# Turning the values of two recurrences with VectorE's 32x32 blocks instead of TensorE, in a fused hybrid decoder layer

## The chip, the cores and the metric

One core of a Trainium2 chip runs the whole layer as one program. The metric is device time in microseconds (us). A time is that of one execution; the kernel before has three, and the profile is of a further execution of its own.

## What is computed

One layer over 320 tokens: 256 of a new sequence (the prompt) and 64 sampled ones (8 requests of 8 tokens), all in float32, with D_MODEL = 2048. Cut to what matters:

```python
proj = jnp.einsum('btd,de->bte', x, w_in)                # all head groups and gates in one projection
h, C, n, m = _mlstm(q, k, v, ig, lf, C0, n0, m0)          # 4 heads, DK 256, DV 512
#   num = einsum('bhts,bhsv->bhtv', s, v) + w_inter * einsum('bhtk,bhkv->bhtv', q, C)
#   den = sum(s) + w_inter * einsum('bhtk,bhk->bht', q, n)
#   C_new = decay * C + einsum('bhs,bhsk,bhsv->bhkv', w_end, k, v)
o, S = _hgrn2(hq, log(f), 1 - f, i, S0)                   # 8 heads, DK 128, DV 256
ya, yb = branch_a @ w_branch_a, branch_b @ w_branch_b
mix = (sig(gate_a) * ya + sig(gate_b) * yb) @ w_out
x1 = layernorm(alpha * x + mix)
y = layernorm(alpha * x1 + relu(x1 @ w_up) ** 2 @ w_down)
```

The outputs are y and the new states C, n, m and S, of the prompt and of the samples.

## The kernel before, in words

**Main stream.** All big projections are one stream of 304 output tiles of 128 columns (`TILES`, made by `tile_list`): the mLSTM projections (v, k, q of a head, between them gates), the HGRN2 projections, then output gates, branches, w_out, and four rounds of w_up and w_down. A tile is [128 columns x 320 tokens] in one PSUM bank and takes 16 steps of 128 along the contraction. Each step is three float32r matmuls (hi x hi, hi x lo, lo x hi: weights and activations are split into a high and a low part), so 48 matmuls to a tile; a half tile of 24 is a unit. Everything is transposed: features lie on partitions, tokens along the free dimension.

**Weights.** `prep` brings a unit of weights from its DMA buffer: ScalarE writes the high part (line 346, `wh<-wr` or `bb<-wr`) and VectorE the low part (line 491). The parts lie in buffer pairs: three at first, eight from w_out on (five wide ones in `bb`); one of the wide ones is lent to the first layer norm meanwhile.

**Recurrences.** Each mLSTM head and each HGRN2 head is a handful of small chains (Python generators): scores, values, states, numerator, samples. The matmuls that contract over tokens need the values with tokens on partitions. So `m_V` turns an mLSTM head's values (128 features x 4 blocks x 320 tokens) by 12 TensorE transposes into PSUM (line 954), from which ScalarE and VectorE make high and low parts; `h_i` turns an HGRN2 head's by 6 (lines 1465 and 1470). The 64 sampled tokens are turned along with the 64 last ones of the prompt, so that they land on partitions 64 to 127. Denominators of the mLSTM are sums over partitions, made as [128 x 1] matmuls with a column of ones (`m_num`, `m_sample`).

**What sets the order.** `Sched` is a planner in Python that runs while the program is built. It has a clock per engine and a cost for each instruction (`act`, `dve`, `pe_r`, `PE_T`), and between the main matmuls `pump` issues the next instruction of any chain whose inputs will be there by its clocks. An instruction of a chain on TensorE goes out only when its input will have been ready for 590 ns by these clocks (`LAT` and `PE_LAT`); VectorE's and ScalarE's at most 900 ns ahead. The result is a fixed order on each engine; on the chip an engine that comes to an instruction too early waits there.

**The end.** After the last tile of w_down come the second layer norm and the prompt's states. `ln_pre` sums the statistics of the first 15 tiles by float32 matmuls with ones (line 352, `bank<-f,ones`) while the last tile runs; `ln_final` adds the last tile; `ln_scale` makes mean M and the factor RS (lines 1838 to 1846 on VectorE, a logarithm and an exponential on ScalarE); `y` subtracts M (line 1960), multiplies by RS (line 1965), ScalarE applies weight and bias (`yb_`, `f3m<-f3m,vec`), and SyncE sends y off. Beside this run the states' matmuls: eight groups of six for C (`m_C`), whose k and v come back from HBM into freed weight buffers through GpSimd's DMA queue (line 1110), and eight pairs for S (`h_S`), each copied out by ScalarE or VectorE.

**Buffers.** SBUF is carved by hand from a few big tiles (`carve`, `carve_h`); regions are reused as stages end.

Of the kernel before, what the change touches and what calls it, by code (L numbers as in the profile page):

```python
# [20 lines left out]
TOK = 320  # L21
# [246 lines left out]

def pe_f(n, m=128):
    return max(212.0 if m == 128 else 162.0, n * 1.66)  # L270
# [39 lines left out]
class Program:  # L310
# [48 lines left out]
    def carve(self):  # L359
# [15 lines left out]
        self.hs = Pool([A(2048) for _ in range(3)])  # L375
# [15 lines left out]
        self.tst = Pool([B(320) for _ in range(2)])  # L391
# [26 lines left out]
        B = Part(self.f2, 4304)  # L418
# [7 lines left out]
    def carve_h(self):  # L426
        C = self.Part(self.pool.tile([128, 5120], F32, name="f3h", tag="f3"))
        qz = C(256)
        self.hqz = Pool([qz])
        self.hyk = Pool([C(128)])  # L430
        for x in (qz, self.ats0, self.hkz0.bitcast(F32), *(y[0:64, 2, :] for y in self.it2)):
            self.nc.gpsimd.memset(x, 0.0)
        X, R = self.Part(self.pool.tile([128, 4096], F32R, name="rxb", tag="rx")), self.Part(self.ra)
        self.bah = Slices([(X if j < 12 else R)(TOK) for j in range(KT)])
        self.bal = Slices([R(TOK) for _ in range(KT)])
        now = self.s.t["pe"]
        self.hs.free.append((now, C(2048)))
# [331 lines left out]
    def rows(self, b):  # L769
# [6 lines left out]
        ig, fx, ax, e, u, lnu, c1, r, lf, bb, a, a1, mt, em = (row() for _ in range(14))  # L776
# [136 lines left out]
    def m_S(self, h):  # L913
# [23 lines left out]
        yield ("act", act(256), lambda: self.A(ss[0:64], f(ss[64:128])))  # L937
        yield post(m["S"])

    def m_V(self, h):  # L940
        nc, v, m = self.nc, self.nc.vector, self.mh[h]
        if h:
            yield wait(self.mh[h - 1]["vst"])
        yield wait(*m["v"])
        vr = m["vr"]
        vhl = yield acq(self.vhl)
        m["vhl"] = vhl
        vh, vl = vhl[:, 0], vhl[:, 1]
        vs = yield acq(self.vs)
        m["vs"] = vs  # L950
        for i, lo in enumerate((0, 128, 192)):
            b = yield acq(self.sbank)
            for j in range(4):
                yield ("pe", PE_T, lambda: nc.tensor.transpose(b[:, 128 * j:128 * j + 128], vr[:, j, lo:lo + 128], self.ident))  # L954

            hi, lo_, x = (vh[:, i, :], vl[:, i, :], b) if i < 2 else (vs[64:128], vs[0:64], b[64:128])
            yield ("act", act(512, True), lambda: self.A(hi, x))
            yield ("dve", dve(512, True), lambda: v.tensor_tensor(lo_, x, hi.bitcast(F32), ALU.subtract))
            yield rel(self.sbank, b)
        yield rel(self.vr, vr)  # L960
# [23 lines left out]
    def m_KW(self, h):  # L984
# [15 lines left out]
        yield ("dve", dve(512), lambda: v.transpose(kw[:, :, 0:256], kw[:, :, 0:256]))  # L1000
# [58 lines left out]
    def m_num(self, h):  # L1059
# [13 lines left out]
        yield ("pe", 212, lambda: self.mm(db[:, 1:2], E[:, 128:256], one, start=True, stop=False))  # L1073
        yield ("pe", 212, lambda: self.mm(db[:, 1:2], E[:, 256:384], one, start=False, stop=True))
        for i in range(2):
            b = yield acq(self.sbank)
            jobs = [(c, s) for c, s in (((0, 0),), ((128, 0), (256, 1)))[i]]
            n = 0
            for c, s in jobs:
                for x, w in ((sh, vh), (sh, vl), (sl, vh)):  # L1080
                    st, sp = n == 0, n == 3 * len(jobs) - 1
                    yield ("pe", pe_r(512), lambda: self.mm(b, x[:, c:c + 128], w[:, s, :], start=st, stop=sp))
                    n += 1
            yield from self.ln_post(h, i, b, db[:, i:i + 1], hb[:, i, :], 128, True)
            yield rel(self.sbank, b)
            yield ("dve", dve(512), lambda: v.transpose(hb[:, i, :], hb[:, i, :]))
# [18 lines left out]
    def m_C(self, h):  # L1105
# [8 lines left out]
        for c in range(2):  # L1114
            if h:
                yield wait(self.ln[1]["fin"])
# [6 lines left out]
            if h < 2 and c == 0:  # L1123
                yield ("dve", dve(512, True), lambda: self.nc.vector.tensor_copy(self.oC[h][:, c, :], b))
            else:
                yield ("act", act(512, True), lambda: self.A(self.oC[h][:, c, :], b))
            yield rel(self.mbank, b)
            yield ("sp", 620, lambda: self.dma(self.d["Cp"][h, :, c, :], self.oC[h][:, c, :]))
        yield rel(self.vx, w)

# [14 lines left out]
    def m_sample(self, h):  # L1145
# [8 lines left out]
        for c in range(2):  # L1154
# [3 lines left out]
            yield ("dve", dve(64), lambda: v.tensor_tensor(by_token(qn, 128 * c, True), qc, n4, ALU.mult))  # L1158
        yield post(m["QW"])
# [13 lines left out]
        for i in range(2):  # L1173
            yield ("pe", pe_r(512), lambda: self.mm(nb, ss[:, 128 * i:128 * i + 128], m["vs"], start=False, stop=i == 1, skip_group_check=True))
        db = yield acq(self.sbank)
        yield ("pe", 212, lambda: self.mm(db[:, 0:1], E[:, 384:512], self.one, start=True, stop=False))
        for c in range(2):
            yield ("pe", 212, lambda: self.mm(db[:, 0:1], qn[:, 128 * c:128 * c + 128], self.one, start=False, stop=c == 1))
# [274 lines left out]
    def h_i(self, h):  # L1453
# [8 lines left out]
        b = yield acq(self.sbank)  # L1462
# [3 lines left out]
        yield ("act", act(512, True), lambda: self.A(it[:, 0:2, :], b.rearrange("p (a v) -> p a v", a=2)))  # L1466
        yield rel(self.sbank, b)
        b = yield acq(self.sbank)
        for j in range(2):
            yield ("pe", PE_T, lambda: nc.tensor.transpose(b[:, 128 * j:128 * j + 128], iv[:, j, 192:320], self.ident))  # L1470
        yield ("act", act(256, True), lambda: self.A(it[64:128, 2, :], b[64:128, 0:256]))
# [3 lines left out]
        yield ("act", act(256, True), lambda: self.A(hi, b[64:128, 0:256]))  # L1475
        yield ("dve", dve(256, True), lambda: v.tensor_tensor(lo, b[64:128, 0:256], hi.bitcast(F32), ALU.subtract))
        yield rel(self.sbank, b)
# [89 lines left out]
    def h_sp(self, h):  # L1567
# [6 lines left out]
        yield ("dve", dve(256), lambda: v.transpose(ks, ks))  # L1574
# [6 lines left out]
    def h_S(self, h):  # L1581
# [8 lines left out]
            b[:, 0:256], x[:, 128 * i:128 * i + 128], x[:, 256 + 256 * i:512 + 256 * i], start=i == 0, stop=i == 1) for i in range(2)])  # L1590
        if h < 4:
# [8 lines left out]
    def h_out(self, h):  # L1600
# [14 lines left out]
        for i in range(2):  # L1615
            yield ("dve", dve(256), lambda: v.transpose(on[:, i, :], on[:, i, :]))
# [127 lines left out]
    def ln_add(self, n, j, z, pre):  # L1744
# [4 lines left out]
        if j < 4:  # L1749
# [7 lines left out]
            if j == 3:  # L1757
                p = yield acq(self.sbank)
                if n == 0:
                    yield from self.total(p, S1, self.lns[0])  # L1760
                else:
                    yield ("pe", pe_f(TOK), lambda: self.mm(p[:, :TOK], self.ones, S1, start=True, stop=True))
# [16 lines left out]
        if j == 15:  # L1779
# [3 lines left out]
            self.hl_free.append((self.s.t["pe"], self.wx[4]))  # L1783
# [6 lines left out]
    def total(self, p, x, hl):  # L1790
        hi, lo = hl[:, 0, :], hl[:, 1, :]
        yield from self.split(x, hi, lo)
        for i, y in enumerate((hi, lo)):
            yield ("pe", 147, lambda: self.mm(p[:, :TOK], self.ones.bitcast(F32R), y, start=i == 0, stop=i == 1))
# [34 lines left out]
    def ln_scale(self, n):  # L1829
# [11 lines left out]
        yield ("dve", dve(TOK, mode=2), lambda: v.tensor_scalar(X, X, 0.0, EPS, ALU.max, ALU.add))  # L1841
        yield ("act", act(TOK), lambda: self.A(RS, X, AF.Ln))
# [109 lines left out]
    def y(self):  # L1952
# [4 lines left out]
        for i in range(KT + 6):  # L1957
# [3 lines left out]
            if i == 5:  # L1961
                yield wait(st["end"])
            if i > 5:
                z = self.acc[:, i - 6, :]
                t = yield ("dve", dve(TOK), lambda: v.tensor_tensor(z, z, self.lnb[4], ALU.mult), (0.0,))
                self.s.spawn(self.yb_(i - 6, z), 0, t)
# [9 lines left out]
    def run(self, pool):  # L1976
# [13 lines left out]
        self.ln = [dict(c=Ev(), end=Ev(), pre=Ev(), m=Ev(), fin=Ev(), s=[Ev() for _ in range(KT)]) for _ in range(2)]  # L1990
# [83 lines left out]
```

## Time and profile before

| what | us |
|---|---|
| median of 3 executions (2310.22 to 2311.4) | 2311.3 |
| the profiled execution's own time | 2310.56 |
| its span, first to last instruction | 2308.7 |
| TensorE busy in it | 2299.2 |
| VectorE busy in it | 1365.3 |
| ScalarE busy in it | 1040.1 |

The granted TensorE clock was 0.999. In the views, PE is TensorE's matmuls and PEld its weight loads, DVE is VectorE, ACT ScalarE, POOL GpSimd, SP SyncE; L352 is line 352. A matmul's duration in a row spans its pipeline, so matmuls overlap in the rows; what one costs is the distance from its start to the next start. The same holds in part for VectorE and ScalarE.

### The profile page before, as it was taken

How to read it: one execution, taken by the hardware profiler on the slowest of the kernel's cores; microseconds unless marked ns; L12 is line 12 of the kernel's file. 1: busy time of each engine (PE TensorE's matmuls, PEld its weight loads, DVE VectorE, ACT ScalarE, POOL GpSimd, SP SyncE). 2: the span in 40 equal slices, each digit the busy share in tenths (PEclk: the TensorE clock that was granted, in tenths of full speed). 3: DMA queues.
4: the chain of work that ended last, by engine and by line, in shares of the span. 5: the costliest groups of instructions: out<-in, count | busy, mean ns of one | idle time of the engine just before them, and what ended most of it. 6: DMA issues, size and time to landing. Idle time of an engine off the chain costs nothing.

```text
span 2308.7 us, 38882 instructions
## 1 busy us (share of the span) xinstructions
PE 2299.2 (100%) x15712; PEld 2258.4 (98%) x15712; DVE 1365.3 (59%) x2333; ACT 1040.1 (45%) x1664; POOL 13.3 (1%) x37
## 2 busy tenths in 40 slices
PE   9999999999999999999999999999999999999998
PEld 9999999999999999999999999999999999999997
DVE  6566667666767776555555767654444444444455
ACT  5443444555556565444433446533433343234333
POOL 0000000000000000000000000000000000000000
PEclk9999999999999999999999999999999999999999
DMA  7677797666556565555555654444444444444466
GB/s 282 209 248 250 236 292 240 204 189 187 183 182 200 170 191 171 176 172 177 170 175 174 213 165 156 146 147 149 152 148 154 146 152 150 148 154 146 154 214 190
DMA packets 214573, 424.94 MB, mean 184 GB/s; under 512 B 83572, under 2 KB 110068, under 8 KB 213368
## 3 DMA queue, kind: packets, MB, share of 16 engines
q1 hardware_dynamic: 209512, 415.97, 55.7%
q0 software_dynamic: 4736, 6.29, 1.1%
q8 instruction: 123, 2.02, 0.4%
q14 instruction: 58, 0.48, 0.1%
q10 hardware_dynamic: 144, 0.20, 0.0%
HBM read 371.48 MB, written 50.90 MB: 183 GB/s over the span
## 4 chain that ended last, share of the span: by engine, by line
PE 99%; ACT 1%; DVE 0%; issue 0%; ACTq 0%; POOL 0%; DVEq 0%; POOLq 0%
PE bank L352 98%; ACT f3m L346 0%; PE bank L954 0%; PE bank L1465 0%; DVE f3m L1960 0%; ACT f L346 0%; PE bank L1470 0%; PE bank L1519 0%; PE bank L1022 0%; PE bank L1626 0%; PE bank L1191 0%; ACT oC L346 0%; ACT oS L346 0%; ACT bb L346 0%; ACT xh L346 0%
## 5 line engine op out<-in xcount | busy, mean ns | idle before, releaser
L352 PE MATMUL bank<-xh,wh 128*128 128x320 f32 (+1 forms) x2432 | 781.3, 322 | 0.0
L352 PE MATMUL bank<-xh,wl 128*128 128x320 f32 (+1 forms) x2432 | 752.2, 310 | 0.0
L352 PE MATMUL bank<-xl,wh 128*128 128x320 f32 (+1 forms) x2432 | 750.0, 309 | 0.0
L491 DVE TENSOR_TENSOR wl<-wr,wh 128x1024 fp32r<-128x1024 f32 x426 | 522.1, 1226 | 381.4 <-ACT wh L346 378.5
L346 ACT ACTIVATE wh<-wr 128x1024 fp32r<-128x1024 f32 x426 | 450.9, 1059 | 514.9 <-PE bank L352 498.1
L352 PEld LDWEIGHTS bank<-xh,wh 128*128 128x128 f32 x2432 | 458.1, 189 | 18.0 <-issue 15.5
L352 PEld LDWEIGHTS bank<-xl,wh 128*128 128x128 f32 x2432 | 458.4, 189 | 3.3
L352 PEld LDWEIGHTS bank<-xh,wl 128*128 128x128 f32 x2432 | 458.0, 188 | 0.2 <-DVE wl L491 0.2
L491 DVE TENSOR_TENSOR bb<-wr,bb 128x1024 fp32r<-128x1024 f32 x176 | 215.7, 1225 | 227.6 <-ACT bb L346 227.5
L346 ACT ACTIVATE bb<-wr 128x1024 fp32r<-128x1024 f32 x176 | 186.4, 1059 | 311.4 <-PE bank L352 293.9
L352 PE MATMUL bank<-xh,bb 128*128 128x320 f32 (+1 forms) x1280 | 285.4, 309 | 0.0
L352 PE MATMUL bank<-rxb,bb 128*128 128x320 f32 x1208 | 276.3, 309 | 0.0
L352 PE MATMUL bank<-ra,wh 128*128 128x320 f32 x988 | 265.9, 309 | 0.0
L352 PE MATMUL bank<-ra,bb 128*128 128x320 f32 x1096 | 264.3, 309 | 0.7 <-DVE ra L1657 0.7
L352 PEld LDWEIGHTS bank<-xh,bb 128*128 128x128 f32 x1280 | 215.0, 188 | 0.0
L352 PEld LDWEIGHTS bank<-rxb,bb 128*128 128x128 f32 x1208 | 204.2, 188 | 0.2
L352 PE MATMUL bank<-xl,bb 128*128 128x320 f32 (+1 forms) x640 | 197.7, 309 | 0.0
L352 PEld LDWEIGHTS bank<-ra,bb 128*128 128x128 f32 x1096 | 187.1, 188 | 1.2 <-DVE ra L1657 0.9
L352 PEld LDWEIGHTS bank<-ra,wh 128*128 128x128 f32 x988 | 176.3, 188 | 0.0
L352 PE MATMUL bank<-rxb,wh 128*128 128x320 f32 x548 | 169.0, 308 | 0.0
L352 PE MATMUL bank<-rxb,wl 128*128 128x320 f32 x548 | 169.0, 308 | 0.0
L352 PEld LDWEIGHTS bank<-xl,bb 128*128 128x128 f32 x640 | 120.4, 188 | 0.2 <-DVE xl L1885 0.2
(262 smaller groups left out, 2195.3 us busy)
## 6 DMA issues: line engine op xcount, KB each, us to landing
wr<-wt SPq DMA_DIRECT2D x602, 512.0 KB, 3.4
rx<-C SPq DMA_DIRECT2D x34, 256.0 KB, 4.8
Cs<-rx SPq DMA_DIRECT2D x34, 256.0 KB, 5.3
f<-C SPq DMA_DIRECT2D x30, 256.0 KB, 5.2
Cs<-f SPq DMA_DIRECT2D x30, 256.0 KB, 5.0
f<-first SPq DMA_DIRECT2D x6, 704.0 KB, 10.3
vD<-ra SPq DMA_DIRECT2D x4, 1024.0 KB, 5.6
f<-S SPq DMA_DIRECT2D x8, 512.0 KB, 6.3
```

Source lines behind the costliest of these rows:

```text
L346: return self.nc.scalar.activation(out, in_, func, **kw)
L352: self.nc.tensor.matmul(*a, **kw)
L491: self.V().tensor_tensor(lo, raw, hi.bitcast(F32), ALU.subtract)
```

## The change

Six things change.

1. `m_V` and `h_i` no longer use TensorE. A new generator, `turn`, issues 24 VectorE transposes per head: each reads 32 partitions of the raw values, turns the 32x32 blocks in them, and writes them to another 32 partitions of an SBUF buffer (`vt` for the mLSTM, `it` itself for HGRN2). For an mLSTM head 16 of them have 256 elements per partition and 8 have 128; for an HGRN2 head 16 have 128 and 8 have 64. The high and low parts are then made from SBUF instead of PSUM; two copies out of PSUM per HGRN2 head on ScalarE are gone. `turn` for an mLSTM head no longer waits for the head before to be done with its stack (`vst`).
2. Denominators: pairs of [128 x 1] matmuls are replaced by an addition on VectorE ahead of one matmul: one matmul less per head in `m_num`, two less in `m_sample`.
3. The second layer norm's early sums use the split form of `total` (high and low part, two float32r matmuls) instead of a float32 matmul: three float32 matmuls become six. Its buffer is the wide weight pair that was lent to the first layer norm, which is no longer given back: seven pairs from then on, not eight.
4. At the end: `y` issues one subtraction of M, then waits until the variance is there (a new event, posted in `ln_scale`) and issues two more before RS; before, it issued six ahead of them. C and S are copied out by generators of their own (`C_out`, `S_out`), all eight C copies by ScalarE; before, two were VectorE's. The second group of the first head's C matmuls now waits for the layer norm's last matmuls.
5. The planner's cost for VectorE transposes is `dve_t(n) = 155 + 1.07 n` ns.
6. Buffers move to make room for `vt`: two sets of HGRN2 buffers instead of three until the mLSTM heads are done, some rows of the gates share memory.

```diff
+def dve_t(n):
+    return 155.0 + 1.07 * n
...
-        self.hs = Pool([A(2048) for _ in range(3)])
+        self.hs = Pool([A(2048) for _ in range(2)])
+        self.hs3 = A(2048)
+        self.vt = Pool([Part(self.f1, 4608).three(3, 512)])
...
     def m_V(self, h):
+        yield wait(*m["v"])
+        vr = m["vr"]
+        vt = yield acq(self.vt)
+        yield from self.turn(vt, vr)
+        yield rel(self.vr, vr)
         if h:
             yield wait(self.mh[h - 1]["vst"])
...
-        for i, lo in enumerate((0, 128, 192)):
-            b = yield acq(self.sbank)
-            for j in range(4):
-                yield ("pe", PE_T, lambda: nc.tensor.transpose(b[:, 128 * j:128 * j + 128], vr[:, j, lo:lo + 128], self.ident))
...
-            yield ("act", act(512, True), lambda: self.A(hi, x))
-            yield ("dve", dve(512, True), lambda: v.tensor_tensor(lo_, x, hi.bitcast(F32), ALU.subtract))
+        for hi, lo, x in ((vh[:, 0], vl[:, 0], vt[:, 0]), (vh[:, 1], vl[:, 1], vt[:, 1]), (vs[64:128], vs[0:64], vt[64:128, 2])):
+            yield ("act", act(512), lambda: self.A(hi, x))
+            yield ("dve", dve(512), lambda: v.tensor_tensor(lo, x, hi.bitcast(F32), ALU.subtract))
...
+    def turn(self, to, x):
+
+        v = self.nc.vector
+        n = x.shape[1]
+        for a in range(4):
+            p = slice(32 * a, 32 * a + 32)
+            col = lambda y: y.rearrange("p (c a k) -> p a c k", a=4, k=32)[:, a]
+            for b in range(4):
+                q = slice(32 * b, 32 * b + 32)
+                i = x[p, :, 0:NP_].rearrange("p c (i b k) -> p b i c k", b=4, k=32)[:, b]
+                o = to[q, 0:2, :].rearrange("p i (c a k) -> p a i c k", a=4, k=32)[:, a]
+                yield ("dve", dve_t(64 * n), lambda: v.transpose(o, i))
+            for b in range(2):
+                o, i = col(to[64 + 32 * b:96 + 32 * b, 2, :]), x[p, :, NP_ + 32 * b:NP_ + 32 * b + 32]
+                yield ("dve", dve_t(32 * n), lambda: v.transpose(o, i))
...
     def m_num(self, h):
-        yield ("pe", 212, lambda: self.mm(db[:, 1:2], E[:, 128:256], one, start=True, stop=False))
-        yield ("pe", 212, lambda: self.mm(db[:, 1:2], E[:, 256:384], one, start=False, stop=True))
+        yield ("pe", 212, lambda: self.mm(db[:, 1:2], E[:, 256:384], one, start=True, stop=True))
...
     def h_i(self, h):
-        for i in range(2):
-            for j in range(2):
-                yield ("pe", PE_T, lambda: nc.tensor.transpose(b[:, 256 * i + 128 * j:256 * i + 128 * j + 128], iv[:, j, 128 * i:128 * i + 128], self.ident))
...
+        yield from self.turn(it, iv)
...
     def ln_pre(self, n):
         for i in range(2):
-            yield ("pe", pe_f(TOK), lambda: self.mm(p[i][:, :TOK], self.ones, self.lnb[i], start=True, stop=False))
+            yield from self.total(p[i], self.lnb[i], self.lns[1 + i], False)
...
     def y(self):
-        for i in range(KT + 6):
+        for i in range(KT + 3):
...
-            if i == 5:
+            if i == 0:
+                yield wait(st["x"])
+            elif i == 2:
                 yield wait(st["end"])
```

The order of three places, word for word, before and after. Names: `xh`, `xl` are the activations' high and low part, `wh`, `wl` the weights', `cst` holds the identity, `ra,ones` is a sum of the HGRN2 scores, `f` with a number are carved buffers.

TensorE, in the second HGRN2 head's time, before:

```order
L352 MATMUL bank_87<-ra,ones 128x480
L1465 MATMUL bank_84<-cst,f_75 128x128
L352 MATMUL bank_83<-xh,wh 128x320
L352 MATMUL bank_83<-xl,wh 128x320
L352 MATMUL bank_83<-xh,wl 128x320
L352 MATMUL bank_87<-ra,ones 128x480
L352 MATMUL bank_83<-xh,wh 128x320
L352 MATMUL bank_83<-xl,wh 128x320
L352 MATMUL bank_83<-xh,wl 128x320
L1465 MATMUL bank_84<-cst,f_75 128x128
```

The same sums of the second head in the change:

```order
L356 MATMUL bank_85<-ra,ones 128x480
L356 MATMUL bank_81<-xh,wh 128x320
L356 MATMUL bank_81<-xl,wh 128x320
L356 MATMUL bank_81<-xh,wl 128x320
L356 MATMUL bank_81<-xh,wh 128x320
L356 MATMUL bank_81<-xl,wh 128x320
L356 MATMUL bank_81<-xh,wl 128x320
L356 MATMUL bank_85<-ra,ones 128x480
L356 MATMUL bank_81<-xh,wh 128x320
L356 MATMUL bank_81<-xl,wh 128x320
```

The transposes of line 1465 are gone from between the main matmuls; nothing stands in their place.

VectorE, before, where the fourth HGRN2 head's values have been turned (line 1476 makes a low part of them from PSUM):

```order
L1359 TENSOR_TENSOR ra<-f_75,ra 128x800
L491 TENSOR_TENSOR wl<-wr,wh 128x1024
L1056 TENSOR_SCALAR misc<-misc 128x1
L1057 TENSOR_TENSOR misc<-misc 128x1
L1288 TENSOR_SCALAR f_76<-bank_83 128x320
L491 TENSOR_TENSOR wl<-wr,wh 128x1024
L1476 TENSOR_TENSOR rh<-bank_84,rh 64x256
L1424 COPY_PREDICATED f_75<-lmask,bank_85 128x320
```

VectorE in the change, while it turns the fourth head's values:

```order
L1156 STREAM_TRANSPOSE f_76<-f_75 32x4x32
L1445 COPY_PREDICATED f_75<-lmask,bank_86 128x80
L497 TENSOR_TENSOR wl<-wr,wh 128x1024
L1419 TENSOR_TENSOR f_75<-f_75 128x40
L1156 STREAM_TRANSPOSE f_76<-f_75 32x4x32
L1466 COPY_PREDICATED f_75<-lmask,bank_88 128x40x4
L1156 STREAM_TRANSPOSE f_76<-f_75 32x4x32
L1664 TENSOR_SCALAR misc<-misc 128x1
L1056 TENSOR_SCALAR misc<-misc 128x1
L1156 STREAM_TRANSPOSE f_76<-f_75 32x4x32
```

The 32-partition transposes stand between other chains' work, mostly one at a time, and the weights' low parts (line 491 before, 497 now) stay among them.

VectorE at the end, before, from the last tile of w_down on (L1960 subtracts M, L1838 makes the variance, L1124 copies a C group, L1965 multiplies by RS):

```order
L1940 TENSOR_TENSOR f3m<-f3m,bank_81 128x320
L1124 COPY oC<-bank_85 128x512
L1960 TENSOR_TENSOR f3m<-f3m,f_76 128x320 x6
L1838 SCALAR_TENSOR_TENSOR f_76<-bank_84,f_76 128x320
L1841 TENSOR_SCALAR f_76<-f_76 128x320
L1844 SCALAR_TENSOR_TENSOR f_76<-f_76 128x320
L1124 COPY oC<-bank_88 128x512
L1845 TENSOR_TENSOR f_76<-f_76 128x320
L1846 SCALAR_TENSOR_TENSOR f_76<-f_76 128x320
L1960 TENSOR_TENSOR f3m<-f3m,f_76 128x320
L1965 TENSOR_TENSOR f3m<-f3m,f_76 128x320
```

The same in the change (L1973 subtracts, L1849 makes the variance, L1980 multiplies):

```order
L1953 TENSOR_TENSOR f3m<-f3m,bank_81 128x320
L1973 TENSOR_TENSOR f3m<-f3m,f_76 128x320
L1849 SCALAR_TENSOR_TENSOR f_76<-bank_86,f_76 128x320
L1852 TENSOR_SCALAR f_76<-f_76 128x320
L1973 TENSOR_TENSOR f3m<-f3m,f_76 128x320 x2
L1857 SCALAR_TENSOR_TENSOR f_76<-f_76 128x320
L1858 TENSOR_TENSOR f_76<-f_76 128x320
L1859 SCALAR_TENSOR_TENSOR f_76<-f_76 128x320
L1973 TENSOR_TENSOR f3m<-f3m,f_76 128x320
L1980 TENSOR_TENSOR f3m<-f3m,f_76 128x320
```

One subtraction stands ahead of the variance instead of six, the two copies of C are off VectorE, and ScalarE has one of its eight between the logarithm and the exponential.

More of the change, by code (lines that the diff above doesn't have):

```diff
@@ L390, in carve @@
         self.qz = Pool([self.qz0])
-        self.tst = Pool([B(320) for _ in range(2)])
+        self.tst = Pool([B(256) for _ in range(2)])
         self.tst2 = B(320)
@@ L436, in carve_h @@
         now = self.s.t["pe"]
-        self.hs.free.append((now, C(2048)))
+        self.hs.free += [(now, C(2048)), (now, self.hs3)]
         self.sb.free += [(now, C.three(4, 256)) for _ in range(2)]
@@ L775, in rows @@
         gs = row(parts=128)
-        ig, fx, ax, e, u, lnu, c1, r, lf, bb, a, a1, mt, em = (row() for _ in range(14))
+        ig, fx, ax, e, u, lnu, c1, bb, a, mt = (row() for _ in range(10))
+        r, lf, a1, em = ax, fx, c1, lnu
         pk = row(712)
@@ L1758, in ln_add @@
                 p = yield acq(self.sbank)
[L1759 to L1762, printed above, removed]
+                yield from self.total(p, S1, self.lns[0])
                 yield ("act", act(TOK, True), lambda: self.A(cb, p[:, :TOK], scale=1.0 / 512))
@@ L1788, in ln_add, with total @@
             self.s.spawn(self.ln_pre(n), 0)
-    def total(self, p, x, hl):
+    def total(self, p, x, hl, stop=True):
         hi, lo = hl[:, 0, :], hl[:, 1, :]
@@ L1793, in total @@
         for i, y in enumerate((hi, lo)):
-            yield ("pe", 147, lambda: self.mm(p[:, :TOK], self.ones.bitcast(F32R), y, start=i == 0, stop=i == 1))
+            yield ("pe", 147, lambda: self.mm(p[:, :TOK], self.ones.bitcast(F32R), y, start=i == 0, stop=stop and i == 1))
     def ln_sum(self, j, z):
@@ L1989, in run @@
         self.vD = [self.dr.tile([128, 2, 2, 512], F32, name=f"vD{j}") for j in range(MH)]
-        self.ln = [dict(c=Ev(), end=Ev(), pre=Ev(), m=Ev(), fin=Ev(), s=[Ev() for _ in range(KT)]) for _ in range(2)]
+        self.ln = [dict(c=Ev(), end=Ev(), pre=Ev(), m=Ev(), fin=Ev(), x=Ev(), s=[Ev() for _ in range(KT)]) for _ in range(2)]
         self.xq, self.xq_ev = [None] * KT, [Ev() for _ in range(KT)]
```

59 lines of the change are left out of this document (25 added, 34 removed).

## Prediction, made before the changed kernel ran

> **What bounds the kernel now.** I read the page's busy shares first, then its chain of work.
>
> ```profile
> span 2308.7 us, 38882 instructions
> PE 2299.2 (100%) x15712; PEld 2258.4 (98%) x15712; DVE 1365.3 (59%) x2333; ACT 1040.1 (45%) x1664; POOL 13.3 (1%) x37
> PE 99%; ACT 1%; DVE 0%; issue 0%; ACTq 0%; POOL 0%; DVEq 0%; POOLq 0%
> ```
>
> The chain that ends last lies 99% on TensorE. Since a busy PE need not be a PE without waits, I cut the span into stages (the columns are PE, PEld, DVE, ACT and POOL busy, then clock and DMA) and looked up what PE waited for.
>
> ```profile
> 40.00:430.00 390.00, 390.00 (x2668) 365.87 (x2667) 257.87 (x500) 173.28 (x286) 2.47 (x7) 1.00 0.79 248
> 430.00:800.00 370.00, 370.00 (x2614) 362.04 (x2614) 263.30 (x653) 210.87 (x462) 2.20 (x6) 1.00 0.60 187
> 1500.00:2284.00 784.00, 784.00 (x5341) 783.02 (x5339) 363.55 (x437) 279.10 (x341) 5.90 (x8) 1.00 0.48 155
> 2284.00:2309.00 25.00, 16.82 (x76) 13.87 (x74) 16.99 (x42) 14.83 (x30) 0.00 (x0) 0.89 0.64 234
> ...
> PE bank L352 <- DVE ra L1657: 0.7, 1, 0.7
> ```
>
> Up to 2284 PE is busy throughout, and the only wait of its matmuls on VectorE in the span is 0.7 us. So there are two pieces: a stream of matmuls in which every matmul taken out shortens the time by its own slot, as long as VectorE and ScalarE go on feeding PE; and a tail of 25 us where VectorE and ScalarE decide. VectorE has 390 - 257.9 = 132 us free in the mLSTM stage (40 to 430) and 370 - 263.3 = 107 us in the HGRN2 stage (430 to 800).
>
> **What leaves the stream.** A slot is the distance from start to start. PE's timeline in the mLSTM stage, first a transpose, then a pair of records of one [128 x 1] matmul; and in the last unit a float32 matmul with ones.
>
> ```profile
> 47.54 0.27 PE L954 MATMUL bank<-cst,f 128*128 128x128 f32 x1
> 47.57 0.39 PE L352 MATMUL bank<-xh,wh 128*128 128x320 f32 x1
> 47.80 0.31 PE L352 MATMUL bank<-xl,wh 128*128 128x320 f32 x1
> 47.95 0.31 PE L352 MATMUL bank<-xh,wl 128*128 128x320 f32 x1
> ...
> 101.18 0.28 PE L352 MATMUL bank<-misc,f 128*128 128x1 f32 x2
> 101.32 0.40 PE L352 MATMUL bank<-xh,wh 128*128 128x320 f32 x1
> 101.56 0.31 PE L352 MATMUL bank<-xl,wh 128*128 128x320 f32 x1
> ...
> 2276.24 0.70 PE L352 MATMUL bank<-f,ones 128*128 128x320 f32 x2
> 2276.53 0.55 PE L352 MATMUL bank<-rxb,bb 128*128 128x320 f32 x1
> 2276.92 0.31 PE L352 MATMUL bank<-ra,bb 128*128 128x320 f32 x1
> ```
>
> A main matmul takes 47.95 - 47.80 = 0.15 us (0.147 over many). From the transpose's start to the second main matmul behind it are 0.26 us; less one main slot, the transpose costs 0.115. Likewise the [128 x 1] matmul costs 0.38 - 0.147 = 0.23, and the float32 one with ones 0.68 - 0.147 = 0.53. The count comes from the code: 4 heads x 12 + 8 heads x 6 = 96 transposes, 4 x (1 + 2) = 12 small matmuls, and 3 float32 ones for 6 float32r ones of a main slot each, the last of which falls behind the stream's end. So the stream loses 96 x 0.115 = 11.0, 12 x 0.23 = 2.8, and 3 x 0.53 - 5 x 0.147 = 0.9 us: **14.7 us**. No main matmul is added or removed.
>
> **What VectorE takes on.** Whole transposes and a partial-partition instruction, from the groups by shape and VectorE's timeline:
>
> ```profile
> L1616 DVE STREAM_TRANSPOSE f<-f 128x256 f32<-128x256 f32 x16 | 6.7, 430 | 0.2 <-ACT f L346 0.2
> L1086 DVE STREAM_TRANSPOSE f<-f 128x512 f32<-128x512 f32 x8 | 5.7, 708 | 0.2
> ...
> 435.55 0.43 DVE L1476 TENSOR_TENSOR rh<-bank,rh 64x256 fp32r<-64x256 f32 x1
> 436.01 0.33 DVE L1445 COPY_PREDICATED f<-lmask,bank 128x160 f32<-128x160 uint8 x1
> 436.25 0.48 DVE L1294 SCALAR_TENSOR_TENSOR f<-f 128x320 f32<-128x320 f32 x1
> ```
>
> The slope is (708 - 430) / 256 = 1.09 ns an element, which gives 291 ns for 128 elements and 221 for 64. No row has a transpose from 32 partitions to 32 others; I take the whole ones as nearest, since all 128 partitions work side by side in them. Then 64 x 430 + 160 x 291 + 64 x 221 ns = 88 us of durations: 37 in the mLSTM stage and 51 in the HGRN2 stage. The occupancy depends on overlap: the instruction behind the 64-partition one starts 0.03 us after its end (435.98 to 436.01), while the next pair overlaps by 0.09. With full overlap 288 instructions cost 88 - 288 x 0.09 = 62 us; with the gap, and the overlap lost by the instruction in front as well, up to 88 + 288 x (0.03 + 0.12) = 131, of it 51 and 80 in the two stages. I take 97 (durations and gaps), since it is nearest to the row with part of the partitions. The free time is 132 and 107 us, less some 8 and 6 by which the stages shrink, so the sum fits at both ends, with 21 us to spare in the HGRN2 stage at the worst. The additions for the denominators are 12 smaller ones, under 6 us even at the last row's 0.48. Reading parts from SBUF instead of PSUM changes no count, and ScalarE loses 16 copies.
>
> The Trainium skill speaks on this, in "VectorE: DVE Perf Modes", "Two Vector instructions with no wait between them": an instruction whose input or output starts in another quarter of the partitions than the last one's is held until all earlier ones have finished. The pair at 436.01 behaves like that, and by this rule nearly every piece of a turn would be held, which speaks against the change. By the rule the turns cost VectorE 97 to 131 us, without it 62 to 88; either is less than its free time.
>
> What queues behind these instructions is the low part of the weights and the chains' own steps. In the new order the weights' low parts keep their places among the pieces, and the pieces stand mostly singly, so a unit waits behind a piece or two of 0.3 to 0.5 us. For PE's side matmuls the order leaves 0.59 us behind a step's planned end. The planner charges the same 430, 291 and 221, plus 0.1 between steps of one chain, but knows no gap and no lost overlap. Where a turn runs among other work, VectorE can fall behind by up to 0.15 x 24 = 3.6 us per head, until it has an idle moment, and PE would wait for the excess over 0.59. Idle moments make up a tenth of the stage even at the worst, so I charge 1 us in all (bounds 0 and 12).
>
> **The tail.** VectorE, ScalarE, PE and SyncE at the end:
>
> ```profile
> 2281.72 1.55 PE L352 MATMUL bank<-bb,wh 128*128 128x512 f32 x6
> 2283.84 0.77 ACT L346 ACTIVATE f<-bank 128x320 f32<-128x320 f32 x2 [0.87 <-PE bank L352]
> 2284.31 2.50 DVE L1960 TENSOR_TENSOR f3m<-f3m,f 128x320 f32<-128x320 f32 x6 [0.32 <-ACT f L346]
> 2286.73 0.48 DVE L1838 SCALAR_TENSOR_TENSOR f<-bank,f 128x320 f32<-128x320 f32 x1
> 2287.61 0.98 ACT L346 ACTIVATE f<-f 128x320 f32<-128x320 f32 x2 [1.24 <-DVE f L1841]
> 2289.03 0.68 DVE L1124 COPY oC<-bank 128x512 f32<-128x512 f32 x1
> 2289.62 0.48 DVE L1845 TENSOR_TENSOR f<-f 128x320 f32<-128x320 f32 x1
> 2291.47 1.46 ACT L346 ACTIVATE f3m<-f3m,vec 128x320 f32<-128x320 f32 x2 [1.01 <-DVE f3m L1965]
> 2292.84 0.58 ACT L346 ACTIVATE oC<-bank 128x512 f32<-128x512 f32 x1
> 2293.31 1.22 ACT L346 ACTIVATE f3m<-f3m,vec 128x320 f32<-128x320 f32 x2
> 2300.35 2.83 ACT L346 ACTIVATE f3m<-f3m,vec 128x320 f32<-128x320 f32 x5
> 2303.90 1.05 SPq L355 DMA_DIRECT2D Sp<-oS  x2
> ```
>
> The mean is ready at 2284.3, yet the variance (L1838) waits behind six subtractions, (2.50 - 0.48) / 5 = 0.40 us each, until 2286.73. With one subtraction ahead it starts at about 2284.9, after 0.15 for the float32r matmul that now precedes the first C group: 1.85 us earlier. The copy inside the chain to RS (2289.03 to 2289.62) saves another 0.59, and its successor on ScalarE between logarithm and exponential costs 0.47. So ScalarE's first output step comes 1.95 us earlier, at about 2289.5. From there ScalarE has hardly a gap until 2303.18, and it gets one more C copy (0.47, from 2292.84 to the next step at 2293.31). Left are about **1.4 us**; what follows ScalarE's end (two DMA issues and the closing) stays. VectorE's remaining 13 subtractions and 16 multiplications at 0.40 end by then too.
>
> **Sum.** 2310.56 - 14.7 - 1.4 + 1.0 = 2295.5 against the profiled execution's own time. The median of the three runs is 0.7 above it, and I carry that over: **2296 us**.
>
> **The rivals.**
> - *The turn's pieces hold up PE.* The gaps and lost overlap that the planner doesn't know come to 288 x 0.15 = 43 us. For it: no row shows such pieces, and a full VectorE has little slack. Against it: the free time above. If about a third reaches PE, 14 us: 2309; a fifth, 9 us: 2304.
> - *A piece is far dearer (slower than before).* If a 32-partition piece is paid like a whole 512-element transpose, 0.70 us, the HGRN2 stage gets 192 x 0.70 = 134 us onto 101 free, PE waits 33 us, and the time is 2328. The point from which this stage alone loses more than the change gains is (101 + 16) / 192 = 0.61 us a piece, twice what I take.
> - *The stream doesn't shorten,* because something beside PE paces it. Then only the tail is left: 2309. Against it: the same 0.147 slot with and without side work, and no waits.
> - *The tail keeps its length.* Seven weight pairs mean that the last head's v may be fetched only when the last unit is done.
>
> ```profile
> 2278.12 0.55 POOL L1110 DMA_DIRECT2D bb<-vD  x1 [5.40 <-PE bank L352]
> bb<-vD POOLq DMA_DIRECT2D x4, 1024.0 KB, 7.7
> 2291.03 1.52 PE L352 MATMUL bank<-bb,wh 128*128 128x512 f32 x6
> ```
>
>   Before, its issue came 3.6 us ahead of the C groups. Issued at their start it lands 8 us later; the seventh group, now the first to need it, starts 9.3 us after them. If it is 2 us late, the time is 2298.
>
> **How the numbers follow.** The forecast with small waits (2292 to 2299) has 0.68, the late v 0.06; PE held up by a fifth to a third of the unknown 0.16; the dearer piece 0.05; no shorter stream 0.05. The range, 2291 to 2306, takes in the bounds of the waits (0 to 12) and leaves out the slow ends, under 2 in 10. A change under 0.2% (4.6 us) can't be told from none here: faster means below 2306.7. That is the forecast, the late v and most of the first rival, 0.87; within the bound lie the rest of it and the stream that isn't shorter, 0.08; slower 0.05.
>
> **What would show it.** PE should show no transposes but those of stacked keys and sampled rows, and waits of under a few us in total up to the last tile; PE's last main matmul should come about 14 us earlier. Pieces of 256, 128 and 64 elements should last about 430, 290 and 220 ns, with gaps of 0.03 between them; VectorE's busy time should rise by some 60 to 130 us. At the end, the variance should start within 1 us of the mean, and ScalarE's first output step about 8 us after the first C group's start. Wrong would be pieces beyond 0.6 us, or PE waits on VectorE of over 5 us.

## The result and the profile after

The changed kernel takes **2302.85 us** (median of 6 runs, 2301.95 to 2304.14) against 2311.22 of the kernel before (6 runs, 2310.22 to 2311.41). The ratio is 0.9967 with a 95% interval of 0.9956 to 0.9977: 8.4 us faster, where the terms of the prediction came to 15.1 (14.7 + 1.4 - 1.0). The profiled execution took 2302.73 us, with a span of 2300.8.

The page of the changed kernel, first its head and then the chain of work that ended last by engine:

```profile
span 2300.8 us, 38921 instructions
PE 2289.6 (100%) x15592; PEld 2246.1 (98%) x15592; DVE 1458.9 (63%) x2634; ACT 1036.6 (45%) x1653; POOL 13.5 (1%) x37
PE 69%; DVE 3%; ACT 1%; issue 0%; ACTq 0%; DVEq 0%
```

PE looks just as full as before, 100%. But the chain now leaves PE several times and runs through VectorE: the long chain on PE alone (99% before) is broken. (The view follows it back to 611.6 us only, where it ends at a wait for VectorE, so the shares add up to 73%.) The stages tell where (PE, PEld, DVE, ACT and POOL busy, then clock and DMA):

```profile
40.00:430.00 390.00, 389.07 (x2631) 363.52 (x2630) 300.42 (x607) 174.85 (x285) 0.00 (x0) 1.00 0.76 246
430.00:800.00 370.00, 367.44 (x2579) 357.43 (x2579) 313.35 (x835) 204.94 (x447) 4.74 (x13) 1.00 0.59 191
```

PE was busy for the whole of both recurrence stages before; now 0.9 and 2.6 us are missing, and VectorE has 43 and 50 us more in them. What PE and its weight loads waited for between 30 and 870 us (us in total, times, longest; rows for "issue" were there before as well and are left out):

```profile
...
PEld bank L356 <- DMA rx<-C: 2.7, 5, 1.1
PEld bank L1530 <- DVE f L987: 2.5, 4, 0.9
...
PE bank L1530 <- DVE f L987: 1.5, 3, 0.7
PE bank L356 <- DVE rh L1488: 1.1, 2, 0.6
PE bank L1212 <- DVE f L1049: 0.7, 1, 0.7
```

Before, PE's matmuls had no wait of 0.2 us or more in this stretch, and its weight loads waited 0.8 us for states. What waits now are the transposes of stacked keys (L1530, L1212), the spread of the turned values (their low part rh, L1488) and the products with mLSTM's state (rx<-C).

A wait shown here is part of a gap only, so I measured **late operands** by slots: over each group of side matmuls, the distance from the main matmul ahead to the second main matmul behind, less the main slots, less what the side matmuls of that kind cost in the trace of before. Here is one of them:

```profile
701.19 0.31 PE L356 MATMUL bank<-xh,wl 128*128 128x320 f32 x1
702.12 0.33 PE L1530 MATMUL bank<-cst,f 128*128 128x128 f32 x1 [0.62 <-DVE f L987]
702.20 0.39 PE L356 MATMUL bank<-xh,wh 128*128 128x320 f32 x1
702.43 0.32 PE L356 MATMUL bank<-xl,wh 128*128 128x320 f32 x1
```

From 701.19 to 702.43 are 1.24 us; two main slots (0.29) and a transpose (0.11) make 0.41: 0.83 late, of which the row shows 0.62. Over the whole trace the sum is **7.9 us** in the changed kernel and 0.2 in the kernel before (where it is the error of the method): 5.5 in ten places behind VectorE and ScalarE, 2.2 in three places behind loads of mLSTM's state, and the rest scattered.

Measured by slots in the same way over the whole trace of before, a removed transpose was worth 0.112 us and a [128x1] matmul 0.227, so 10.7 + 2.7 left the recurrences, and 0.9 the last units. The first C group, which starts the tail, shows the balance:

```profile
2275.70 1.54 PE L356 MATMUL bank<-bb,wh 128*128 128x512 f32 x6
```

It started at 2281.72 before, 6.0 us later. The terms give -14.3 + 7.9 + 0.4 (this execution's first side-work unit started 0.4 us later) = -6.0. The rest came off the tail, from this start to the span's end: 26.98 us before, 25.10 now.

### The profile page after: what moved, and what is told of

It is laid out like the page before. It is cut to its first block, busy times and chain, and to the rows that moved or that the text cites. A ratio compares the mean times of both kernels' runs of the same rounds, so it can differ in the third digit from the quotient of the medians.

```text
span 2300.8 us, 38921 instructions
## 1 busy us (share of the span) xinstructions
PE 2289.6 (100%) x15592; PEld 2246.1 (98%) x15592; DVE 1458.9 (63%) x2634; ACT 1036.6 (45%) x1653; POOL 13.5 (1%) x37
## 4 chain that ended last, share of the span: by engine, by line
PE 69%; DVE 3%; ACT 1%; issue 0%; ACTq 0%; DVEq 0%
PE bank L356 69%; DVE wl L497 1%; ACT wh L350 0%; DVE f L1156 0%; DVE f L1445 0%; ACT f L350 0%; DVE f3m L1973 0%; DVE f3m L1980 0%; ACT f3m L350 0%; DVE f L1159 0%; DVE f L1315 0%; DVE f L1316 0%; DVE f L1631 0%; DVE f L1698 0%; DVE f L1309 0%
## 5 line engine op out<-in xcount | busy, mean ns | idle before, releaser
L356 PE MATMUL bank<-xh,wl 128*128 128x320 f32 (+1 forms) x2504 | 774.8, 310 | 0.0
L356 PE MATMUL bank<-xl,wh 128*128 128x320 f32 (+1 forms) x2504 | 772.2, 309 | 0.0
L356 PE MATMUL bank<-xh,bb 128*128 128x320 f32 (+1 forms) x1136 | 253.8, 309 | 0.0
L356 PE MATMUL bank<-rxb,bb 128*128 128x320 f32 x1088 | 249.0, 309 | 0.0
L356 PEld LDWEIGHTS bank<-xh,bb 128*128 128x128 f32 x1136 | 191.0, 188 | 0.0
L356 PE MATMUL bank<-rxb,wh 128*128 128x320 f32 x608 | 187.5, 308 | 0.0
L356 PE MATMUL bank<-rxb,wl 128*128 128x320 f32 x608 | 187.5, 308 | 0.0
L356 PEld LDWEIGHTS bank<-rxb,bb 128*128 128x128 f32 x1088 | 184.2, 187 | 0.0
L356 PE MATMUL bank<-xl,bb 128*128 128x320 f32 (+1 forms) x568 | 175.5, 309 | 0.0
L356 PE MATMUL bank<-bb,wh 128*128 128x320 f32 (+1 forms) x536 | 119.0, 313 | 0.0
```

Source lines behind the costliest of these rows:

```text
L356: self.nc.tensor.matmul(*a, **kw)
```

## Experiments

Two theories were put to test. **A**: a piece of a turn costs VectorE more than the planner charges; in busy stretches VectorE falls behind the planned order, and PE, which takes its matmuls in that order, waits. **B**: the new order itself (other pools, a moved place of the state loads) brings operands late, whatever a piece costs. Each time below is a median against the kernel before on the same chip (2310.8 to 2311.0 us).

**The same program with every piece in one quarter.**

```
-                i = x[p, :, 0:NP_]...
-                o = to[q, 0:2, :]...
+                i = x[0:32, :, 0:NP_]...
+                o = to[0:32, 0:2, :]...
```

> Every piece of both turns now reads the first 32 partitions and writes the first 32 partitions, as every full instruction starts there too. Left out: the turned values of the other three quarters are wrong. The program's order is that of the changed kernel, instruction for instruction; only the start quarters differ. Theory A (a piece is held behind the instruction in front and holds the one behind, so VectorE falls behind the plan and PE waits for late operands, 7.8 us in all in the changed kernel): the gaps of 0.03 us around pieces become overlaps of about 0.08, late operands fall below 2 us, and the time to 2296 to 2298. Theory B (the new order itself puts operands and state loads late, whatever a piece costs): the time stays within 2302 to 2304.

Measured: **2296.78 us** (ratio 0.9940, 0.9928 to 0.9953), late operands 1.6 us, of which 1.4 behind state loads. VectorE's timeline around a piece, in the changed kernel and then in this one, at the same place of the program:

```profile
697.99 1.22 DVE L497 TENSOR_TENSOR wl<-wr,wh 128x1024 fp32r<-128x1024 f32 x1
699.13 0.44 DVE L1323 TENSOR_SCALAR f3h<-f3h,misc 128x320 f32<-128x320 f32 x1
699.49 0.15 DVE L1664 TENSOR_SCALAR misc<-misc 128x1 f32<-128x1 f32 x1
699.64 0.31 DVE L1156 STREAM_TRANSPOSE f<-f 32x128 f32<-32x128 f32 x1
699.97 0.52 DVE L1445 COPY_PREDICATED f<-lmask,bank 128x80 f32<-128x80 uint8 x1
700.52 0.33 DVE L1466 COPY_PREDICATED f<-lmask,bank 128x160 f32<-128x160 uint8 x1
...
701.77 0.29 DVE L987 TENSOR_TENSOR f<-f,f 128x128 fp32r<-128x128 f32 x1
```

```profile
692.66 1.22 DVE L497 TENSOR_TENSOR wl<-wr,wh 128x1024 fp32r<-128x1024 f32 x1 [0.38 <-ACT wh L350]
693.81 0.44 DVE L1323 TENSOR_SCALAR f3h<-f3h,misc 128x320 f32<-128x320 f32 x1
694.16 0.15 DVE L1664 TENSOR_SCALAR misc<-misc 128x1 f32<-128x1 f32 x1
694.23 0.29 DVE L1156 STREAM_TRANSPOSE f<-f 32x128 f32<-32x128 f32 x1
694.45 0.47 DVE L1445 COPY_PREDICATED f<-lmask,bank 128x80 f32<-128x80 uint8 x1
...
695.99 0.27 DVE L987 TENSOR_TENSOR f<-f,f 128x128 fp32r<-128x128 f32 x1
```

Above, the piece at 699.64 starts when the instruction ahead has ended, and the next one starts 0.02 us after the piece's end; below, the one behind starts 0.07 us before the piece has ended. From the weights' low part (wl) to the subtraction on which the late transpose hangs (L987) are 3.78 us against 3.33. And below VectorE stands idle for 0.38 us ahead of wl: it waits for ScalarE, it has caught up. The order is the same in both, so B can't explain the 6.1 us; what is left lies at the state loads. The Trainium skill, "VectorE: DVE Perf Modes", "Two Vector instructions with no wait between them", says that a Vector instruction starts only after all earlier ones have ended when its input or output starts in another group of 32 partitions than the last one's. Both timelines agree with it: the gap of 0.03 us in front of a piece (median of 250) becomes an overlap of 0.08. The changed kernel also shows it without any edit: the first piece of each turn reads and writes the first quarter, and these 12 overlap the full instruction ahead by 0.08 us, while the pieces that stay within one of the other quarters have the gap of 0.03, like those that move.

**Charging the piece in the plan.** Four kernels differ from the changed one in one number of the planner only, in both lines of the turn (the order changes with it):

```
-                yield ("dve", dve_t(64 * n), lambda: v.transpose(o, i))
+                yield ("dve", dve_t(64 * n) + 100, lambda: v.transpose(o, i))
```

with +150, +100, +50 and -100 ns.

> The planner charges each piece 0.15 us more, which is the gap of 0.03 us and the lost overlap of 0.11 us that the changed kernel's trace shows. Theory A: the plan then keeps step with VectorE, PE's late operands fall from 7.8 us to under 3, and the time comes to 2297 to 2299. Theory B: late operands stay at 6 to 9 us in other places, 2301 to 2305.

> The planner charges each piece 0.10 us more instead of 0.15. With 0.15 more the plan itself ran out of time: the last head's turn ended so late that PE was made to stand for 6 us ahead of the tile at 921 us, where the next stage needs the head's buffers. With 0.10 more the plan has no such halt. Theory A (pieces are dearer than planned): late operands fall from 7.8 us to 2 to 4, 2297 to 2300. Theory B (the late operands are an accident of the order): 2301 to 2305.

> Half of the charge that gave 2296.6: 0.05 us more per piece. Theory A: late operands between 7.8 and 2.6, about 5 us, 2299 to 2300. Theory B: anywhere from 2297 to 2305.

> The planner charges each piece 0.10 us less than in the changed kernel, 0.25 less than the trace shows that it costs with its neighbour. Theory A: VectorE falls behind further, late operands 11 to 14 us in place of 7.8, 2306 to 2309. Theory B (each order has its own luck): 2297 to 2305.

| charge per piece, ns | time, us | ratio to before, 95% interval | late operands, us |
|---|---|---|---|
| -100 | 2309.45 | 0.9993 (0.9984 to 1.0002) | 14.6 |
| 0 (the change) | 2302.85 | 0.9967 (0.9956 to 0.9977) | 7.9 |
| +50 | 2298.98 | 0.9952 (0.9938 to 0.9965) | 4.5 |
| +100 | 2296.58 | 0.9939 (0.9925 to 0.9952) | 2.6 |
| +150 | 2309.32 | 0.9992 (0.9983 to 1.0001) | 15.0 |

Up to +100 the late operands fall with the charge, as A has it. Counting the groups that are over 0.1 us late, those at state loads come to 3.0, 2.2, 3.8 and 0.7 us (from -100 to +100), without a trend; it is the rest, behind VectorE and ScalarE, that falls, from 11 over 5.5 to under 2 us at +50 and +100. At +100 the view of waits has no matmul of PE's between 30 and 870 us (0.2 us is the least that it lists), and the chain of work is on PE again:

```profile
PE 98%; DVE 0%; ACT 0%; DMA 0%; issue 0%; SPq 0%; ACTq 0%; DVEq 0%
```

At -100 the longest waits are of the same kinds as in the changed kernel, but more of them and longer (the first row is again the spread of the turned values):

```profile
PE bank L356 <- ACT f L350: 4.5, 3, 1.7
PE bank L1530 <- DVE f L987: 2.1, 1, 2.1
PE bank L1641 <- ACT f L350: 1.1, 3, 0.5
PE bank L356 <- DMA f<-C: 0.7, 1, 0.7
```

At +150 I was wrong. The waits there have another cause (first two rows of PE's waits, 30 to 930 us):

```profile
PE bank L1641 <- ACT f L350: 5.3, 1, 5.3
PE bank L356 <- DVE ra L964: 1.7, 1, 1.7
```

The 5.3 us lie at 926 us, ahead of the tile "hg" (the first one of HGRN2's output gates), before which the planner waits until every HGRN2 head has ended. The pieces of a head are one chain of 24 steps, so the higher charge makes the planned chain 24 x 0.15 = 3.6 us longer per head; the last heads no longer end in time, and the plan itself lets PE stand. A second one, 2.0 us of slots at 90 us (the wait for L964), lies where the plan waits for a head's buffers. Without these two, 7 us of late operands are left, 3.7 of them at state loads, where A had under 3; so the scatter between orders is a few us as well, and the rows of the table are no fine scale.

A halt also costs more than its own length. TensorE's rows behind the long one:

```profile
926.64 0.69 PE L1641 MATMUL bank<-cst,f 128*128 128x128 f32 x2 [5.32 <-ACT f L350]
...
927.39 0.47 PE L356 MATMUL bank<-xl,wh 128*128 128x320 f32 x1
927.66 0.47 PE L356 MATMUL bank<-xh,wl 128*128 128x320 f32 x1
```

A main slot is 0.27 us here in place of 0.15. The granted clock is 0.50 from 926.5 to 929.9 us and 1.00 behind that; ten such slots add some 1.3 us (an estimate from these rows). The same is seen behind the halt at 90 us. Between 30 and 2270 us of all these profiles it follows four waits of TensorE, of 1.74, 2.10, 5.32 and 6.77 us; a wait of 1.67 us was not followed by it.

The order of +150 also gives wrong values: y is off by 3 to 6% and the samples' S by 0.3%. Which step uses its data at the wrong time is open. Its time is that of this order, and not of a kernel that can be used.

**More slack behind every step.**

```
-PE_LAT = 450.0
+PE_LAT = 900.0
```

> The planner leaves 0.45 us more behind each step before it lets PE use its result (0.90 in place of 0.45). Theory A: late operands of up to 0.9 us are mostly covered, state loads of up to 1.3 us not fully: late operands 2 to 4 us, 2298 to 2300. Theory B: no better, 2302 to 2304, since side work only moves.

> The planner leaves 0.70 us behind a step in place of 0.45 (0.90 had cost a halt of 7.4 us at 916 us, as the side work came too late for the next stage); with 0.70 the plan has no halt. Theory A: 0.25 us off each of some eleven late operands, 7.8 to about 5 us, 2300; some side work ends later. Theory B: 2302 to 2304.

With 900: 2307.06 us (0.9983, 0.9974 to 0.9992), late operands 11.1, of which 7.4 in one place, again the last head's transposes ahead of "hg" (at 916 us), with a clock of 0.50 for 6.8 us from 920 us on; this order gives wrong values, too (y by 1 to 2%, the samples' S by 9%). With 700: **2297.72 us** (0.9943, 0.9931 to 0.9956), late operands 3.4, of which 1.5 at state loads. The same waits go when PE is given its operand later in the plan, as long as the plan makes its deadline. That is what A says, from the other side.

**Each turn alone, and neither.** In each kernel one or both of the functions m_V and h_i are those of before; all else stays changed.

> Only HGRN2's values are turned on VectorE; mLSTM's go back to TensorE's transposes (48 of 0.112 us, 5.4 us, come back into the stream), while pools and all else stay as changed. Theory A: the late operands before 430 us (0.9 for a transpose and 2.2 for state loads) go, those behind it (4.6) stay: 2302.9 + 5.4 - 3.1 = 2305. Theory B (pools and order): the 2.2 us for state loads stay, 2307.

> Only mLSTM's values are turned on VectorE; HGRN2's go back to TensorE's transposes (48 of 0.112 us, 5.4 us, come back). Theory A: the late operands of the HGRN2 stage (4.6 us) go, those before 430 us (3.2) stay: 2302.9 + 5.4 - 4.6 = 2303.7. Theory B: late operands of some 7 us stay somewhere: 2307.

> All of the change but the two turns: mLSTM's and HGRN2's values go through TensorE's transposes as before (10.7 us come back). From the terms: 12 small matmuls 2.7, float32 sums 0.9, the end 1.7, so 5.3 us under the kernel before, 2305.5, with no late operands. If the pools, the denominators or the order brought late operands of their own (Theory B), 2308 to 2312.

Only HGRN2's turn: 2304.58 us (0.9973, 0.9962 to 0.9984), late operands 4.2, all of those above 0.15 us behind 430 us and none at state loads. Only mLSTM's: 2302.85 us (0.9965, 0.9952 to 0.9977), late operands 4.0, the long ones all before 430 us: 0.9 at the transpose L1212 and 3.3 in three places at state loads (other groups scatter below zero). Neither turn: 2304.56 us (0.9973, 0.9963 to 0.9984), late operands 1.8, nearly all at two state loads (1.5 and 0.4). So each turn makes the late operands behind VectorE of its own stage. The change without the turns gains 6.4 us by the medians, and both turns as they stand add only 1.7; with the charge of +100 they add 8.0. (2305.5 was expected of the kernel without turns; its seven executions lie between 2304.01 and 2306.30.)

The late state loads are not shown to come from the turns, nor from the order. The kernel with HGRN2's turn alone and the one with neither have the same order on TensorE, VectorE, ScalarE and SyncE up to 420 us; the profiled execution of the first has no late state load there, that of the second has 1.9 us. So up to 2 us of them come and go between executions, and since each sum of late operands is from one execution, differences below that say nothing.

**Pieces in groups.**

```
-                yield ("dve", dve_t(64 * n), lambda: v.transpose(o, i))
...
+            for lo, hi in [(0, 4), (4, 6)]:
+                cost = sum(dve_t(64 * n if k < 4 else 32 * n) + 20 for k in range(lo, hi)) + 150
+                yield ("dve", cost, lambda: [v.transpose(*y) for y in g[lo:hi]])
```

> The pieces are issued four and two at a time, back to back, and the planner charges such a group 0.02 us more per piece and 0.15 more per group, about what the changed kernel's trace shows for neighbouring pieces (0.318 us from start to start for 128 elements). Theory A: VectorE loses overlap twice per quarter instead of six times, plan and chip agree, late operands under 3 us, 2296 to 2299; the group of 1.3 to 1.9 us in front of other steps may add a wait where the plan has none. Theory B: 2301 to 2305.

Measured: 2296.30 us (0.9937, 0.9925 to 0.9950), late operands 2.4. This order gives wrong values as well (y by 12 to 14%; the cause is open), so it counts for the waits only. VectorE's timeline has four pieces of 128 elements in one row of 1.26 us:

```profile
608.39 0.41 DVE L1370 TENSOR_TENSOR f<-f 128x240 f32<-128x240 f32 x1
608.83 1.26 DVE L1162 STREAM_TRANSPOSE f<-f 32x128 f32<-32x128 f32 x4
610.13 0.41 DVE L1371 TENSOR_TENSOR f<-f 128x240 f32<-128x240 f32 x1
```

That is 0.315 us a piece, for which VectorE's busy time is 1447.5 us in place of 1458.9. It is no faster than the charge of +100 by more than the runs scatter, which agrees with A: most was in the plan and not in the work.

The fastest of these kernels that computes the layer is the changed one with +100 per piece: 2296.58 us, 14.3 us below the kernel before and 6.3 below the change as made.

## Why the prediction was right or wrong

The measured 2302.85 us lies within the stated range of 2291 to 2306, but outside the forecast with small waits, 2292 to 2299, which had a chance of 0.68. It lies within the range only because that took in the bounds of the waits; the time comes nearest to the first rival's 2304, and that rival had 0.16. By slots PE's late operands behind VectorE and ScalarE came to 5.5 us, so the sign of being wrong, waits of over 5 us, appeared. Two of the prediction's sums are off by one, without weight here: a stream that doesn't shorten gives 2310 (2311.3 - 1.4), and waits of 12 us give 2307.

**What leaves the stream: right.** 14.7 us were forecast (11.0 + 2.8 + 0.9); by slots 10.7 + 2.7 + 0.9 = 14.3 left it.

**What VectorE takes on: the price was right, my choice between its ends was not.** Durations were to be 430, 291 and 221 ns, 88 us in all; the groups by shape show

```profile
L1156 DVE STREAM_TRANSPOSE f<-f 32x128 f32<-32x128 f32 x96 | 29.0, 303 | 2.3
L1156 DVE STREAM_TRANSPOSE f<-f 32x256 f32<-32x256 f32 x64 | 27.9, 436 | 1.5
...
L1159 DVE STREAM_TRANSPOSE f<-f 32x64 f32<-32x64 f32 x48 | 11.4, 238 | 1.0
```

303 ns stand for all 160 of 128 elements and 238 for all 64 of 64: 91.6 us. The gap of 0.03 us was right as well, and so was the overlap lost in front of a piece: wl takes 1.142 us from start to start when a full instruction follows and 1.256 when a piece does, 0.114 more (0.12 was the bound). That holds 0.083 of lost overlap and the gap in front; the gap behind the piece comes on top, 0.145 in all. With 238 held pieces behind a full instruction (the 12 first ones are not held) and 38 behind another piece, where the gap is 0.014, that makes 91.6 + 238 x 0.145 + 38 x 0.014 = 127 us. I took 97; the upper end, 131, was nearly the true one. For the total this changed nothing, as 127 fits the free time, too. VectorE's busy time, which leaves out the gaps, rose by 93.6 us, where 60 to 130 were forecast.

**What queues behind: the step that failed.** "Idle moments make up a tenth of the stage even at the worst, so I charge 1 us in all (bounds 0 and 12)". PE's late operands came to 7.9 us (6.3 of them due to the held pieces, by the run with every piece in one quarter), which is nearly all of what the forecast sum lacked: 7.9 - 1.0 = 6.9 of the 7.2 us between 2295.5 and the profiled 2302.73. (Of the rest, 0.4 is what the stream lost less and 0.4 the later start, and the tail gave some tenths more.) The mechanism had been written down there, 3.6 us of arrears per head against 0.59 of slack, and then was averaged away. An average over the stage says nothing of a stretch in which nothing is idle: VectorE's timeline of the changed kernel shows no gap of 0.15 us or more from 669.20 to 702.33 us, and the chain of work runs through it from 672 to 702. A part of that chain (start, us, what):

```profile
675.19 0.21 DVE f L1367
675.39 0.03 issue
675.42 0.24 DVE f L1159
675.66 0.03 issue
675.69 0.48 DVE f L1570
...
701.86 0.21 DVE f L987
```

The 0.03 us of "issue" on both sides of a piece (L1159) are its gaps; L987 is the subtraction that PE waits for at 702.12.

The first rival, "the turn's pieces hold up PE", gave 2304 for a fifth of 43 us; it is what happened, with 6.3 of 43, a seventh. The condition that I put against it, free time in the stage, was the wrong one. By the runs with other charges the right one is whether the planner's charge is what the piece costs, and that could be read beforehand from the row at 435.98 to 436.01 and the planner's own figures.

**The tail: right.** Forecast were 1.4 us. VectorE and ScalarE at the end, first VectorE, then ScalarE:

```profile
2278.30 0.49 DVE L1973 TENSOR_TENSOR f3m<-f3m,f 128x320 f32<-128x320 f32 x1 [2.05 <-ACT f L350]
2278.70 0.48 DVE L1849 SCALAR_TENSOR_TENSOR f<-bank,f 128x320 f32<-128x320 f32 x1
```

```profile
2277.82 0.77 ACT L350 ACTIVATE f<-bank 128x320 f32<-128x320 f32 x2
...
2283.31 0.66 ACT L350 ACTIVATE f3m<-f3m,vec 128x320 f32<-128x320 f32 x1 [0.22 <-DVE f3m L1980]
...
2293.25 2.29 ACT L350 ACTIVATE f3m<-f3m,vec 128x320 f32<-128x320 f32 x4
```

The variance (L1849) starts 0.40 us behind the start of the first subtraction, where it was 2.42 before (2284.31 to 2286.73). ScalarE's first output step comes 7.6 us after the C groups' start at 2275.70, where 8 were forecast and 9.75 were seen before, and ScalarE ends 19.8 us after that start in place of 21.5: 1.6 us, and 1.9 at the span's end. In the kernels above, the time from the last main matmul to the span's end lies between 25.0 and 26.9 us (27.1 before), so this gain carries an uncertainty of some tenths.

**The other rivals.** A piece of 0.61 us or more did not appear: about 0.45 us with what it holds up. The stream did shorten. The late load of the last head's v did no harm: PE shows no wait in the tail for it.

## What to carry to other kernels

An engine that is idle for 15 to 23% of a stage (VectorE here) can still make a full engine wait, where an order fixed ahead charges less than the chip takes: compare the charge with the distance from start to start, with the neighbours' lost overlap in it, and not the load with the free time. When late operands appear with unchanged work, correct the planner's charge before you touch the work: here one constant was worth 6.3 us, three quarters of what the change itself gained (8.4). And look how far the last chain is from its deadline first, since a charge or a slack a little higher turned the gain into a halt, with TensorE's clock halved behind it.

## What the runs showed of the hardware

A 32-partition transpose itself takes 13 to 17 ns longer in the changed kernel (436, 303 and 238 ns) than with every piece in the first quarter, where all full instructions start:

```profile
L1156 DVE STREAM_TRANSPOSE f<-f 32x128 f32<-32x128 f32 x96 | 27.8, 290 | 0.1
L1156 DVE STREAM_TRANSPOSE f<-f 32x256 f32<-32x256 f32 x64 | 27.0, 422 | 0.4
L1159 DVE STREAM_TRANSPOSE f<-f 32x64 f32<-32x64 f32 x48 | 10.6, 221 | 0.1
```

The move is not the reason: in the changed kernel a piece of 128 elements lasts 293 ns from the first quarter to the first, but 304 when it stays within another one. What counts is that it starts in another quarter than the instruction ahead. Between two pieces in a row the gap is 0.014 us, half of that next to a full instruction. Why the state loads of mLSTM land up to 2 us late in some executions is open: no run here separated the smaller pool of state buffers and their place on SyncE's queue from what differs between executions.
